# Fused matmul, GELU, matmul by fast bilinear products: issuing the x transposes of block 2 earlier and reordering the sums that read them

## Chip, cores and metric

The kernel runs on one core of one Trainium2 chip. The metric is device time in microseconds (us) of one launch. TensorE (PE) multiplies matrices into PSUM, VectorE (DVE) does elementwise work, ScalarE (ACT) does activations and copies, GpSimd (POOL) and SyncE (SP) mostly issue DMAs here.

## What is computed

```python
# x: (16, 512, 768)  w1: (768, 3072)  b1: (3072,)  w2: (3072, 768), all float32
y = np.matmul(x, w1) + b1
y = 0.5 * y * (1.0 + erf(y / np.sqrt(2.0)))
return np.matmul(y, w2).astype(np.float32)
```

x is read as 8192 rows of 768. The first product with its GELU gives g of 8192 x 3072, which goes to DRAM as fp16 (`gd`), and the second product reads it back.

## The kernel before

Both products are made by bilinear schemes that need fewer block products than the plain method: sums and differences of blocks of x (or g) are multiplied with sums and differences of blocks of w1 (or w2), 20 block products to a *unit*, and the results are combined out of PSUM. Each unit is given by tables: `P1_XOPS` and `P1_WOPS` say which sums to make, `P1_ORD` in which order the 20 products run and in which of 6 PSUM chains each accumulates, `P1_OPS` how PSUM values are copied ('C'), combined ('A') and finished ('F', which ends in a GELU on ACT, a tile of g, and a store of it by SP). The `F` variants of the tables are for the first unit of a block.

**Phase 1** handles the first 512 rows with plain matmuls woven into block 0, and the rest in six *blocks* (`BLK`): blocks 0 and 1 take three times 256 rows, blocks 2 to 5 three times 512. A block of 256s has three units, each over two column groups of w1; a block of 512s has six units. Every unit of phase 1 takes PE about 13 us. **Phase 2** (second product) starts near 455 us and keeps PE busy to the end.

The x rows of block *b* reach PE in three steps:

1. **Cast.** POOL issues a DMA that reads 256 rows of x from DRAM and writes them as fp16 to `xd` in DRAM (`x_cast1`, line 643). Such casts wait for a *marker*: a tiny DVE memset (line 371) put behind a named product of PE, which POOL reads first (line 361). So a cast starts when PE has come to that place.
2. **Transpose.** SP issues a DMA transpose of these 256 rows into SBUF (`load_x`, line 684): three for block 1, six for each block of 512s. Two SBUF areas (`O_XA`, `O_XB`) serve the blocks in turn, so the transposes of block *b* must wait for the last product of block *b-2*.
3. **Sums.** DVE makes 13 sums of the transposed thirds (`x_sums`, recorded under line 333 with tile `ar` and 1536 elements for blocks 2 to 5). Sums 1 and 3 need the second third or parts of it, sum 2 the first, sum 4 the second and third. The first sum reads what transposes 3 and 4 bring, the second transposes 1 and 2, the fourth transposes 3 to 6.

The order of instructions on each engine is not written by hand. A small planner (`Sched`) keeps a model clock for every engine and for the DMAs, takes the task that can start first, and emits it. It runs when the program is built; on the chip each engine then follows its fixed order and waits on semaphores. A task's *due* time puts it behind or ahead of others; `order=` names tasks after which it may be emitted; `lag` is the model's pause after a dependence before it can start; and a DMA is modelled to end two microseconds after its bytes have passed. The model's times decide the order, never the running time itself.

In `load_x` the mark behind which transpose *k* of block *b* is emitted is a store of the block before: for block 2, store 2 + 3*k* of block 1. A few lines carry what the change touches:

```python
            m0, dm = {1: (22, 4), 2: (2, 3)}.get(b, (8, 5))
            mark = blk_stores[b - 1][m0 + dm * k:m0 + dm * k + 1]
            ...
                order=mark, nbytes=256 * K * 2, bulk=1, lag=1.0 if b == 2 else 8.0)
```

The casts of block 3 are issued while blocks 1 and 2 run: the places of their markers are the list `at` and, for the last two, the loop under `if b == 2`. `prods[u][i]` is product *i* of unit *u* of the block just recorded. Stores of g share 13 SBUF buffers (`NGST`), PSUM results on their way share 7 (`NV`)[...].

Of the kernel before, what the change touches and what calls it, by code (L numbers as in the profile page):

```python
# [44 lines left out]
LAT = 0.13  # L45
WIN = 30.0
URG = 1.0


class Val:  # L50
    __slots__ = ("pool", "slot", "prods", "left", "last")
# [37 lines left out]


class Task:
    __slots__ = ("eng", "fn", "nd", "outs", "reads", "alloc", "frees", "due", "key", "end",
                 "deps", "nbytes", "bulk", "lag", "lock", "gen")


class Sched:
# [10 lines left out]
        self.port = 0.0  # L107
        self.pe_ideal = 10.0

    def add(self, eng, fn, reads=(), alloc=None, makes=None, after=(), frees=None, due=None, nbytes=0, bulk=0, order=(), lag=LAT, lock=False):  # L110

        t = Task()
        t.eng, t.fn, t.alloc, t.due, t.nbytes = eng, fn, alloc, due, nbytes
        t.bulk = bulk
        t.lag = lag
        t.lock = lock
        t.end = None
        t.gen = False
        self.key += 1
        t.key = self.key  # L120
        t.outs = []
        t.reads = list(reads)
        t.frees = list(reads) if frees is None else list(frees)
        for v in t.frees:
            v.left += 1
        if makes is None:
            makes = [alloc] if alloc is not None else []
        deps = set(after)
        for v in t.reads:
            deps.update(v.prods)  # L130
        for v in makes:
            v.prods.append(t)
        t.deps = [d for d in deps]
        t.nd = 0
        for d in list(t.deps) + list(order):
            if d.end is None:
                d.outs.append(t)
                t.nd += 1
        self.left += 1
        if "PE" in eng:  # L140
            self.pe.append(t)
            t.due = self.pe_ideal
            self.pe_ideal += eng["PE"]
        elif t.nd == 0:
            self._ready(t)
        return t
# [20 lines left out]
    def run(self, until=None):  # L167
        drift = 0.0
        while self.left:
            best = None  # L170
            if self.pp < len(self.pe):
                drift = max(self.t["PE"] - self.pe[self.pp].due, 0.0)
            if self.pp < len(self.pe):
                t = self.pe[self.pp]
                if t.nd == 0:
                    r = self._start(t, "PE")
                    if r is not None:
                        best = (r, 0, "PE", t)
            for e in ("DVE", "ACT", "POOL", "SP"):
                fg = None  # L180
                bg = None
                now = self.t[e]
                for t in self.avail[e]:
                    r = self._start(t, e)
                    if r is None:
                        continue
                    if t.due is None:
                        c = (r, t.key, t)
                        if e == "DVE" and "ACT" in t.eng and self.t["ACT"] < r + 0.8 and self.pp > 40:
                            continue  # L190
                        if fg is None or c[:2] < fg[:2]:
                            fg = c
                    elif e != "POOL" and r > t.due + drift - URG:
                        c = (r, t.due - 1e9, t)
                        if fg is None or c[:2] < fg[:2]:
                            fg = c
                    elif e == "POOL" or "POOL" not in t.eng or r > t.due + drift - WIN:
                        if e == "POOL" and len(t.eng) > 1 and r + t.eng[e] > t.due + drift - 0.5:
                            continue
                        c = (r > now + 0.2, t.due, t.key, r, t)  # L200
                        if bg is None or c[:3] < bg[:3]:
                            bg = c
                if bg is not None and (fg is None or bg[3] + 0.5 * bg[4].eng[e] <= fg[0]):
                    c = (bg[3], 1, e, bg[4])
                elif fg is not None:
                    c = (fg[0], 1, e, fg[2])
                else:
                    continue
                if best is None or c[0] < best[0]:
                    best = c  # L210
            assert best is not None, "no task can start"
            r, _, e, t = best
            d = t.eng[e]
            if t.alloc is not None and t.alloc.pool is not None:
                t.alloc.slot = t.alloc.pool.take()
            t.fn(e)
            if t.lock and e != "ACT":
                self.port = r + d
            if t.nbytes:
                self.t[e] = r + d  # L220
                self.dma[t.bulk] = max(self.dma[t.bulk], r + d) + t.nbytes / (270e3, 250e3, 200e3)[t.bulk]
                t.end = self.dma[t.bulk] + 2.0
            else:
                t.end = self.t[e] = r + d
            t.eng = {e: d}
            if e == "PE":
                self.pp += 1
            else:
                for q in self.avail.values():
                    if t in q:  # L230
                        q.remove(t)
            for v in t.frees:
                v.left -= 1
                v.last = max(v.last, t.end)
                if v.left == 0 and v.pool is not None:
                    v.pool.put(v.last + LAT, v.slot)
            for o in t.outs:
                o.nd -= 1
                if o.nd == 0 and "PE" not in o.eng:
                    self._ready(o)  # L240
            self.left -= 1
# [3 lines left out]
def kernel(  # L245
# [9 lines left out]
    B, M, K = x.shape  # L255
# [38 lines left out]
    def a32(off, n):  # L294
        return ar[:, off // 2: off // 2 + 2 * n].bitcast(FP32)
# [353 lines left out]
            (j, y) for j in range(3) for y in range(0, n, 256))]  # L649

    for h in range(3):
        gate = [(w1f[2], a32(O_WF + 2 * 6144, 2))] if h == 0 else []
        x1l.append(S.add({"POOL": 0.95}, lambda e, h=h, gate=gate: gated(gate, lambda: nc.gpsimd.dma_start(
            out=a16(O_XN + 6144 + h * 3072, 2 * K).rearrange("p (s k) -> p s k", k=K),
            in_=xr[:, 4 + 2 * h:6 + 2 * h, :])), alloc=x1n[h], reads=[g[0] for g in gate], nbytes=2 * P * K * 4,
            order=x1l[-1:]))
# [19 lines left out]
    def load_x(b):  # L676

        r0, n = BLK[b]
        for k, (j, y) in enumerate((j, y) for j in range(3) for y in range(0, n, 256)):
            a, z = r0[j] + y, r0[j] + y + 256  # L680
            c = xcv[b, k]
            m0, dm = {1: (22, 4), 2: (2, 3)}.get(b, (8, 5))
            mark = blk_stores[b - 1][m0 + dm * k:m0 + dm * k + 1]
            S.add({"SP": 1.6}, lambda e, a=a, z=z, j=j, y=y: nc.sync.dma_start_transpose(
                out=x_third(b, j)[:, :, y:y + 256], in_=xd[a:z, :]), reads=[c], makes=[xsv[b][j], xsv[b][3 + j]],
                after=blk_last[b - 2] if b > 1 else w1op[0] + plain_mm[:8],
                order=mark, nbytes=256 * K * 2, bulk=1, lag=1.0 if b == 2 else 8.0)


    def plain_pair(p):  # L690
# [137 lines left out]
    for b in range(len(BLK)):  # L828
        p1_block(b)
        at = {0: [prods[1][0], prods[1][10], plain_mm[16], plain_mm[20], prods[2][0], prods[2][6]] if b == 0 else [],  # L830
              1: [prods[1][3], prods[1][12], prods[2][3], prods[2][12]]}.get(b, [p[10] for p in prods])
        if b == 2:
            for r, t in zip(x_rows(3)[4:], (prods[0][3], prods[0][12])):
                x_cast1(*r, gate=marker(t), order=poolq)
        if b + 2 < len(BLK):
            for r, t in zip(x_rows(b + 2), at):
                x_cast1(*r, gate=marker(t), order=poolq)
        if b + 1 < len(BLK):
            load_x(b + 1)

        if b == len(BLK) - 2:
            for k in range(12):
                t, h = divmod(k, 2)
                t = (3, 2, 0, 4, 1, 5)[t]
                g = marker(prods[k // 2][(3, 13)[k % 2]])
                poolq.append(S.add({"POOL": 1.0}, lambda e, t=t, h=h, g=g: gated(g, lambda: nc.gpsimd.dma_start(
                    out=w2d[t][:, 4 * h:4 * h + 4, :], in_=w2b[t // 2, t % 2][:, 4 * h:4 * h + 4, :])),
                    reads=[g[0][0]], makes=[], nbytes=2 * P * 1536 * 2, order=poolq[-1:]))
                w2cast[t].append(poolq[-1])
# [192 lines left out]
```

## Time and profile before

| | us |
|---|---|
| median of 13 runs | 885.16 |
| lowest and highest run | 880.65, 893.58 |
| the profiled execution, its own time | 881.16 |
| its span in the trace | 879.4 |
| PE busy | 856.6 |
| DVE busy | 662.4 |
| ACT busy | 447.5 |
| POOL busy | 55.9 |

The trace is of one execution. Its span runs from the first to the last instruction; its own time is 1.8 us longer. "Busy" is the sum of an engine's instructions; idle time of an engine that is not the bottleneck costs nothing. A *releaser* is what ended a wait, inferred from semaphores. In the timelines a bracket holds the idle time of the engine before an instruction and its releaser. A DMA issue on SP or POOL takes the queue's time; its data land later. "PEclk" or "clock" is the share of full speed that TensorE was granted.

### The profile page before, as it was taken

How to read it: one execution, taken by the hardware profiler on the slowest of the kernel's cores; microseconds unless marked ns; L12 is line 12 of the kernel's file. 1: busy time of each engine (PE TensorE's matmuls, PEld its weight loads, DVE VectorE, ACT ScalarE, POOL GpSimd, SP SyncE). 2: the span in 40 equal slices, each digit the busy share in tenths (PEclk: the TensorE clock that was granted, in tenths of full speed). 3: DMA queues.
4: the chain of work that ended last, by engine and by line, in shares of the span. 5: the costliest groups of instructions: out<-in, count | busy, mean ns of one | idle time of the engine just before them, and what ended most of it. 6: DMA issues, size and time to landing. Idle time of an engine off the chain costs nothing.

```text
span 879.4 us, 14440 instructions
## 1 busy us (share of the span) xinstructions
PE 856.6 (97%) x5024; PEld 487.5 (55%) x5024; DVE 662.4 (75%) x1104; ACT 447.5 (51%) x809; POOL 55.9 (6%) x120
## 2 busy tenths in 40 slices
PE   7999979999999999999998999999999999999997
PEld 4766865444444444434445666666666666666664
DVE  3988769688787876797889886687666678666663
ACT  6787858678778777768891222222222222222221
POOL 3101001000000111121100000000000000000000
PEclk9999999999999999999999999999999999999999
DMA  9999798985787699876693546664546665445612
GB/s 257 217 233 198 183 204 184 212 208 154 176 198 193 157 220 233 193 238 206 233 308 116 162 165 216 207 199 155 156 157 205 206 212 168 162 162 169 215 64 72
DMA packets 154312, 166.51 MB, mean 189 GB/s; under 512 B 55504, under 2 KB 146384, under 8 KB 147664
## 3 DMA queue, kind: packets, MB, share of 16 engines
q1 hardware_dynamic: 135040, 134.91, 51.1%
q0 software_dynamic: 16112, 30.68, 19.7%
q8 instruction: 39, 0.64, 0.3%
q10 hardware_dynamic: 3088, 0.01, 0.2%
q14 instruction: 33, 0.27, 0.1%
HBM read 99.10 MB, written 90.83 MB: 216 GB/s over the span
## 4 chain that ended last, share of the span: by engine, by line
PE 85%; DMA 5%; DVE 4%; ACT 3%; issue 2%; SPq 1%; DVEq 0%; ACTq 0%
PE ps L980 47%; PE ps L805 34%; DMA ar<-xd 3%; PE ps L698 3%; DVE vt L333 2%; ACT ar L503 2%; DVE ar L333 1%; DMA ar<-in_w_dram 1%; SPq L508 1%; ACT vt L338 1%; ACT ar L338 0%; DMA gd<-ar 0%; DVE vt L340 0%; DVE vt L331 0%; PE ps L468 0%
## 5 line engine op out<-in xcount | busy, mean ns | idle before, releaser
L980 PE MATMUL ps<-ar 128*128 128x384 f16 x2560 | 416.6, 326 | 2.5 <-DVE vt L333 1.3
L805 PE MATMUL ps<-ar 128*128 128x512 f16 (+1 forms) x2160 | 395.4, 344 | 10.8 <-DVE vt L340 4.8
L980 PEld LDWEIGHTS <-ar 128*128 128x128 f16 x2560 | 250.5, 98 | 168.6 <-issue 3.1
L805 PEld LDWEIGHTS <-ar 128*128 128x128 f16 x2160 | 211.7, 98 | 194.3 <-issue 16.0
L333 DVE TENSOR_TENSOR ar<-ar 128x1024 f16<-128x1024 f16 (+2 forms) x397 | 273.2, 715 | 18.6 <-DMA ar<-xd 11.0
L338 ACT ACTIVATE vt<-ps 128x384 f32<-128x384 f32 (+1 forms) x288 | 151.4, 537 | 266.0 <-PE ps L980 247.0
L333 DVE TENSOR_TENSOR vt<-ps,vt 128x512 f32<-128x512 f32 (+1 forms) x221 | 139.2, 643 | 106.6 <-ACT vt L338 75.3
L503 ACT ACTIVATE ar<-vt,b1t 128x512 f16<-128x512 f32 (+1 forms) x288 | 177.7, 645 | 73.1 <-DVE vt L333 68.2
L333 DVE TENSOR_TENSOR vt<-vt,ps 128x512 f32<-128x512 f32 (+1 forms) x189 | 125.0, 663 | 39.6 <-PE ps L805 24.9
L503 ACT ACTIVATE ar<-ps,b1t 128x512 f16<-128x512 f32 (+1 forms) x168 | 97.5, 619 | 8.4 <-PE ps L698 3.3
L333 DVE TENSOR_TENSOR vt<-vt 128x384 f32<-128x384 f32 (+1 forms) x80 | 48.5, 607 | 12.3 <-ACT vt L338 9.5
L338 ACT ACTIVATE ar<-vt 128x384 f32<-128x384 f32 x32 | 16.7, 523 | 71.7 <-DVE vt L333 71.7
L361 POOL COPY scr<-mkt 1x1 f32<-1x1 f32 x45 | 14.9, 332 | 351.4 <-DVE mkt L371 351.4
L698 PE MATMUL ps<-ar 128*128 128x512 f16 x144 | 33.4, 393 | 2.4 <-DVE ar L340 2.1
L333 DVE TENSOR_TENSOR ar<-vt 128x384 f32<-128x384 f32 x48 | 26.8, 559 | 3.4 <-ACT vt L338 1.2
L331 DVE SCALAR_TENSOR_TENSOR vt<-vt,ps 128x512 f32<-128x512 f32 x30 | 20.6, 686 | 11.5 <-ACT vt L338 9.7
L338 ACT ACTIVATE ar<-ar 128x768 f16<-128x768 f16 (+3 forms) x27 | 24.5, 930 | 5.3 <-DMA ar<-in_x_dram 3.4
L698 PEld LDWEIGHTS <-ar 128*128 128x128 f16 x144 | 14.3, 101 | 20.4 <-issue 2.3
L331 DVE SCALAR_TENSOR_TENSOR ar<-vt,ps 128x384 f32<-128x384 f32 x32 | 17.7, 554 | 5.0 <-PE ps L980 0.7
L340 DVE COPY vt<-ps 128x512 f32<-128x512 f32 x24 | 16.5, 689 | 1.8 <-PE ps L805 1.7
L643 POOL DMA_DIRECT2D xd<-in_x_dram x27 | 13.3, 494 | 5.8 <-issue 3.8
L333 DVE TENSOR_TENSOR ar<-ps,vt 128x384 f32<-128x384 f32 x16 | 8.9, 558 | 4.6 <-PE ps L980 3.3
(25 smaller groups left out, 75.6 us busy)
## 6 DMA issues: line engine op xcount, KB each, us to landing
gd<-ar SPq DMA_DIRECT2D x384, 128.0 KB, 4.0
ar<-gd SPq DMA_DIRECT2D x42, 1024.0 KB, 7.4
out_dram<-ar SPq DMA_DIRECT2D x128, 192.0 KB, 3.6
xd<-in_x_dram POOLq DMA_DIRECT2D x27, 384.0 KB, 6.5
ar<-gd POOLq DMA_DIRECT2D x6, 1024.0 KB, 6.2
w2d<-in_w_dram POOLq DMA_DIRECT2D x12, 384.0 KB, 6.8
ar<-w2d POOLq DMA_DIRECT2D x12, 384.0 KB, 5.4
ar<-in_w_dram SPq DMA_DIRECT2D x4, 768.0 KB, 9.1
```

Of the source, the lines that this page charges most:

```text
L331: eng.scalar_tensor_tensor(out=o, in0=a, scalar=-1.0, in1=b, op0=ALU.mult, op1=ALU.subtract)
L333: eng.tensor_tensor(out=o, in0=a, in1=b, op=ALU.add if op == "+" else ALU.subtract)
L338: nc.scalar.activation(out=o, in_=a, func=ACTF.Copy, scale=float(sg))
L340: eng.tensor_copy(out=o, in_=a)
L361: nc.gpsimd.tensor_copy(out=o[0:1, 0:1], in_=ap[0:1, 0:1])
L503: ft.append(S.add({"ACT": act_ps(n)}, lambda e, y=y: nc.scalar.activation(out=a16(O_GST + g.slot * 1024 + y * n * 2, n), in_=src[1]()[:, y ...
L508: stores.append(S.add({"SP": 0.45}, lambda e: nc.sync.dma_start(out=gd[un][:, t:t + k, c0:c0 + n], in_=a16(O_GST + g.slot * 1024, 512).rea ...
L643: gate, lambda: nc.gpsimd.dma_start(out=xd[a:z, :], in_=xf[a:z, :])),
L698: nc.tensor.matmul(out=ps[:, bv.slot, :], lhsT=a16(O_WS[u // 2] + q * 3072 + kc * 512 + u % 2 * 256, P), rhs=a16(O_XT0 + kc * 1024, 512), ...
L805: nc.tensor.matmul(out=ps[:, bk, y * n:(y + 1) * n], lhsT=w1_ap(u + y, w, kt), rhs=xa[:, kt * n:(kt + 1) * n], start=(first and kt == 0 an ...
L980: nc.tensor.matmul(out=ps[:, bk, 0:NB], lhsT=xa[:, j, :], rhs=a16(w2v[w][j // 4].slot + j % 4 * NB * 2, NB), start=(first and j == 0), sto ...
```

## The change

Three constants are added, and the planner's tasks get a field for how long after its bytes a DMA is modelled to end.

- The transposes of block 2 are marked by the last store of block 0 (the first two), then by stores 1, 3, 5 and 7 of block 1, where before it was stores 2, 5, 8, 11, 14 and 17. Their model lag goes from 1.0 to 0.5.
- The model lets a transpose of block 2 end 8 us after its bytes, of blocks 3 and later 12 us, where it was 2. It moves the sums in DVE's order.
- The casts of block 3 are gated by seven places of which the first is dropped: three in block 1's units 1 and 2, three in block 2's units 0 and 1, where it was four and two.

```diff
+M2 = 2
+L2 = 8.0
+L3 = 12.0
...
-                t.end = self.dma[t.bulk] + 2.0
+                t.end = self.dma[t.bulk] + t.late
...
-        gate = [(w1f[2], a32(O_WF + 2 * 6144, 2))] if h == 0 else []
+        gate = [(w1f[1], a32(O_WF + 6144, 2))] if h == 0 else []
...
             mark = blk_stores[b - 1][m0 + dm * k:m0 + dm * k + 1]
+            if b == 2:
+                mark = (blk_stores[0][-1:] + blk_stores[1])[M2 * max(k - 1, 0):][:1]
...
-                order=mark, nbytes=256 * K * 2, bulk=1, lag=1.0 if b == 2 else 8.0)
+                order=mark, nbytes=256 * K * 2, bulk=1, lag=0.5 if b == 2 else 8.0, late=(0, 2.0, L2)[b] if b < 3 else L3)
...
-              1: [prods[1][3], prods[1][12], prods[2][3], prods[2][12]]}.get(b, [p[10] for p in prods])
+              1: [prods[1][12], prods[2][3], prods[2][12]]}.get(b, [p[10] for p in prods])
         if b == 2:
-            for r, t in zip(x_rows(3)[4:], (prods[0][3], prods[0][12])):
+            for r, t in zip(x_rows(3)[3:], (prods[0][3], prods[0][12], prods[1][3])):
                 x_cast1(*r, gate=marker(t), order=poolq)
```

The instruction orders that the two programs are built to: PE's and POOL's are the same in both. On SP the six transposes of block 2 stand, counted in stores of g after block 0's last one, behind 0, 1, 2, 5, 9 and 12 stores, where it was 3, 6, 9, 12, 15 and 18. On DVE the sums of blocks 2 to 4 stand elsewhere among the evictions of PSUM; ACT takes one w1 copy and one PSUM copy from DVE.

One line belongs to none of these parts: at the start POOL reads a word of a piece of w1, which SP loads in four pieces (line 416), before it issues its first load of x (line 653). With the change it reads the second piece instead of the third.

More of the change, by code (lines that the diff above doesn't have):

```diff
@@ L91 @@
 class Task:
-    __slots__ = ("eng", "fn", "nd", "outs", "reads", "alloc", "frees", "due", "key", "end",
+    __slots__ = ("eng", "fn", "nd", "outs", "reads", "alloc", "frees", "due", "key", "end", "late",
                  "deps", "nbytes", "bulk", "lag", "lock", "gen")
@@ L108, in __init__, with add @@
         self.pe_ideal = 10.0
-    def add(self, eng, fn, reads=(), alloc=None, makes=None, after=(), frees=None, due=None, nbytes=0, bulk=0, order=(), lag=LAT, lock=False):
+    def add(self, eng, fn, reads=(), alloc=None, makes=None, after=(), frees=None, due=None, nbytes=0, bulk=0, order=(), lag=LAT, lock=False, late=2.0):
         t = Task()
@@ L116, in add @@
         t.lock = lock
+        t.late = late
         t.end = None
```

## The prediction

> **What bounds the kernel now.** I began with busy time: TensorE (PE) works 97% of the span, so only moments in which its queue stands still, or its clock is cut, can be won. The page's chain of waits has three things beside matmuls that this change touches: `DMA ar<-xd` 3%, `DVE ar L333` 1% and `SPq L508` 1%. Next I asked who waited for whom between 116 and 126 us, where block 1's third unit starts:
>
> ```profile
> PEld L805 <- issue: 5.0, 1, 5.0
> PE ps L805 <- DVE vt L340: 4.8, 1, 4.8
> DVE ar L333 <- DMA ar<-xd: 4.2, 1, 4.2
> ```
>
> PE stood 4.8 us for a VectorE (DVE) copy, and DVE stood 4.2 us for a transpose of x. DVE's timeline there (start, length, what, idle before):
>
> ```profile
> 113.43 0.69 DVE L333 TENSOR_TENSOR vt<-ps,vt 128x512 f32<-128x512 f32 x1
> 115.93 0.69 DVE L333 TENSOR_TENSOR vt<-vt,ps 128x512 f32<-128x512 f32 x1 [1.81 <-PE ps L805]
> 120.83 1.83 DVE L333 TENSOR_TENSOR ar<-ar 128x1536 f16<-128x1536 f16 x2 [4.21 <-DMA ar<-xd]
> ...
> 123.77 0.95 DVE L333 TENSOR_TENSOR ar<-ar 128x1536 f16<-128x1536 f16 x1
> 124.65 0.68 DVE L340 COPY vt<-ps 128x512 f32<-128x512 f32 x1
> ```
>
> The two instructions at 120.83 are x sums of block 2, which no matmul needs for another 16 us (the third unit's 13.1 us from 117.6, with the stall and the slow clock, end near 137). Behind them in DVE's queue is the copy that PE needs. The SyncE (SP) queue's timeline shows why the transpose was late:
>
> ```profile
> 97.05 3.67 SPq L508 DMA_DIRECT2D gd<-ar  x4
> 100.89 1.41 SPq L684 DMA_TRANSPOSE ar<-xd  x1
> 102.39 1.55 SPq L508 DMA_DIRECT2D gd<-ar  x3
> 104.05 1.41 SPq L684 DMA_TRANSPOSE ar<-xd  x1
> ...
> 107.23 1.43 SPq L684 DMA_TRANSPOSE ar<-xd  x1
> ...
> 110.40 5.41 SPq L684 DMA_TRANSPOSE ar<-xd  x1
> ```
>
> The sums wait for the fourth transpose, issued at 110.40. Pieces of the chain of waits, in order of time:
>
> ```profile
> 78.31 11.13 PE ps L805 x102
> ...
> 110.40 10.33 DMA ar<-xd
> ...
> 125.39 6.36 PE ps L805 x42
> ```
>
> It took 10.33 us. After the stall 42 matmuls took 6.36 us; at the rate before it (11.13/102 = 0.109 us) they take 4.58, so 1.78 us more went to a slow clock. The busy times by stage agree (length, PE, PEld, DVE, ACT, POOL, then clock, DMA share, GB/s):
>
> ```profile
> 104.50:117.60 13.10, 13.08 (x121) 11.57 (x120) 8.99 (x16) 10.41 (x27) 1.32 (x4) 1.00 1.10 193
> 117.60:130.70 13.10, 8.29 (x63) 6.61 (x61) 8.10 (x13) 5.51 (x14) 0.66 (x2) 0.87 1.04 217
> ```
>
> DMA issues between 101 and 108 us (transposes alone with stores), then between 108.5 and 115.5 (casts of block 3 beside them; the first line of that is the casts' queue):
>
> ```profile
> ar<-xd SPq DMA_TRANSPOSE x3, 4.2
> ```
> ```profile
> q0 software_dynamic: 32, 0.39, 44.4%
> ...
> ar<-xd SPq DMA_TRANSPOSE x2, 8.7
> ```
>
> Landing takes 4.2 us without a cast, 8.7 beside one.
>
> **What the skill says.** The Trainium skill, "TensorE: Matmul & The Clock Gate", Part 1: after an idle window of about 3.4 us the clock is halved for at least one window. The trace agrees: clock 0.87 over 13.1 us is 3.4 us at half speed. "DMA: Bandwidth & Descriptors", Queues, rings and completion order: an engine alternates between queues packet by packet. A large packet then holds small ones up; the casts' 32 packets for 0.39 MB, and 8.7 against 4.2 us, fit this. "PSUM — Partial Sum Buffer", Engine vs sequencer instructions: VectorE's queue is strictly first in, first out; above, ready evictions stood behind the waiting sums.
>
> **The change part by part.** I also compared the two built instruction orders: PE's and POOL's are the same, so the casts move by their markers alone.
>
> 1. *Transposes of block 2 on SP.* The store at 97.05 is block 0's last; three stores then stood ahead of the first transpose. Now it goes at 97.55 (97.05 and 0.5 for one store). The tile it overwrites is free: block 0's last unit, 120 matmuls of 0.109 us from 78.31, ends near 91.4. A transpose costs SP 1.5 us (1.41 and the gap), a store 0.53 (1.55/3 and the gap). The new order has 5 stores before the fourth transpose and 12 before the sixth: 97.55 + 3x1.5 + 5x0.53 = 104.7 us and 97.55 + 5x1.5 + 12x0.53 = 111.4 us, against 110.40 and 122.80. At 4.2 us the fourth lands near 109. The engines are nearly full: six transposes (0.39 MB) and 12 stores (0.13 MB) are 3.9 MB, and 101 to 108 us moved 211 GB/s, hence 18.6 us from 97.6: the sixth lands at 115.6 to 116.5. Stores passed by a transpose leave 1 to 4.5 us later. That is hidden by the 13 g buffers: ScalarE (ACT) fills one per 1.1 us (12 per unit of 13.1 us), a reserve of 14 us, against up to 4.5 of delay and about 3 of landing (2.9 in that window). If the reserve were used up, ACT would wait, then DVE's buffers, then PE, us for us.
>
> 2. *Casts of block 3.* The one at 108.63 goes; from 113.9 on, each gate serves the cast before it, and a sixth falls into block 2's second unit. Block 3's first transpose starts at 153.0 and the sixth at 184.0, the last moved cast lands near 155 (its gate lies 3 products into a unit that starts near 145; landing 6.7): nothing waits, nor the stores behind on SP. What is left is the cast at 113.9, which can still meet the sixth transpose: 4.5 us (8.7 less 4.2), at most 121.
>
> 3. *Sums on DVE.* Same 13 sums per block (0.87 us each back to back). In block 1 the first two now stand one eviction earlier, right after the one at 113.43, so they need the fourth transpose at 114.1: 5 us of reserve. Then: two sums to 115.9, eviction to 116.6, sum to 117.5, two evictions to 118.8, and the fourth sum, which needs the sixth transpose: expected 116, at most 121, so a hold of 0 to 2.2 us. I take 0.5. The copy goes from DVE to ACT, which does three in a row there; in the trace that pattern after seven sums in one boundary cost PE 0.87 us (140.40 to 141.26). It stays at block 2's start, and at this boundary, with six sums, I put 0 to 0.9, taken 0.3.
>
> 4. *Later blocks.* The first sums of blocks 3 and 4 come a unit (13 us) later. In before they held DVE for 6.8 us (11.0 for all six waits on `ar<-xd`, less 4.2) in five small waits, but PE showed no gap there. Gain in the profiled execution 0; in others, where a transpose lands later, up to a few us. They are packed 3, 4, 5 to a unit: 4x0.87 = 3.5 us against 4.1 us that DVE has free in a unit (13.1 less 8.99), so it fits. Block 5's sums move nearly not at all.
>
> 5. *Gate of the first x load on POOL.* It waits for w1's second piece (landed 13.24) instead of the third (15.50), so POOL's three x loads and the w1 loads behind them start 2.26 us earlier, while the third and fourth pieces are still in flight. The x loads landed at 21.4, 23.8 and 26.5, and PE transposed them at 25.0, 26.6 and 28.1 without a gap: nothing to win. The third piece, cast by DVE at 15.83, may come up to a us later; PE takes it up near 18.7, ready near 16.4 before, so 1 us of delay is covered. The fourth (18.70, cast at 20.87) has 2 us. I take 0, from 0 to 0.8.
>
> 6. One w1 copy goes from DVE (0.35 us) to ACT (0.84 us) near 59 us; ACT idles 0.9 us there: nothing; without that gap, 0.84 us at most.
>
> Sum for the profiled execution (881.16 us; span 879.4): -4.80 - 1.78 + 0.5 + 0.3 = -5.8, hence 875.4; bounds 874.6 (no new waits) and 880.2 (2.2, 0.9, 0.8 and another half-clock window of 1.7). The median of the runs is 4.0 above the profiled one. I let half of this surplus go, since late transposes are its likely cause and part 4 gives them a unit more: 875.4 + 2 = **877.4 us**. If all of it stays, 879.4.
>
> **Rivals.**
> A, as above, 0.74: 873 to 880 at the median. The lower end is 874.6 less the 0.87 gap, should it go, and the 0.5 by which the fastest run (880.65) undercuts the profiled one.
> B, the wait moves: the sixth transpose lands with the 10.33 us of the worst one, at 121.7; DVE stands 2.9 us, PE about as long, and pays a half window: 881.16 - 6.6 + 2.9 + 1.7 = 879.2, 883 at the median. For it: the cast at 113.9 is still there. Against: most of that transpose's packets are ahead of the cast's. 0.12, half of it within the bound.
> C, slower: DVE falls behind. Sums packed 3, 4, 5 into the last units before blocks 3 and 4 make evictions late, and PE waits at both starts and at block 2's. It decides once DVE's free 4.1 us in a unit are overdrawn by about 2 us (a store pass or an ACT delay would do): 3 x (2 + 1.7 for the clock) = 11, so 881.2 - 5.8 + 11 = 886, 890 at the median. For it: the 0.87 us gap after seven sums. Against: block 2's first unit took ten sums and lost just that. 0.08.
> D, nothing arrives earlier, as the DMA engines are full anyway: 881, median 885. Against: from 101 to 108 us slices at 340 GB/s stand beside slices under 100, so there is room. 0.06.
>
> **Numbers.** About 0.5% (4.4 us) is what a measurement can tell from no change. Faster: 0.71 of A and half of B, 0.77; same: 0.03, 0.06 and D's 0.06, 0.15; slower 0.08. The range 873 to 882 takes A and the faster half of B.
>
> **What would show it.** Right: the first transpose of block 2 near 97.6, the fourth landing before 114; no PE gap near 120; a clock of 1.00 between 117 and 131; DVE's wait on `ar<-xd` falling from 11.0 us to under 3. Wrong: a DVE wait on the sixth transpose over 2 us near 119, or PE gaps over 1 us at the starts of blocks 2 to 4.

## The result

| | before | after |
|---|---|---|
| median, us | 885.49 | 874.89 |
| lowest and highest run | 879.93, 898.65 | 873.51, 876.47 |
| the profiled execution, its own time | 881.16 | 875.95 |
| its span | 879.4 | 874.1 |

The medians are of all 48 and 11 runs; the ratio leaves out every run more than 1.5% above the fastest of its kernel. It is 0.9884 (after to before), with a 95% interval of 0.9861 to 0.9907. The forecast was 877.4 us (873 to 882) at the median and 875.4 for the profiled execution. Two things happened: a stall went, and so did nearly all of the spread. The runs of before cover 19 us, those of after 3. Long runs became rare, though, and did not vanish: of six later runs of after one took 881.32 us.

### The profile after

First the waits between 113 and 124 us, where before had the 4.8 us stall (columns: engine, line waited for, releaser; then us in total, times, longest):

```profile
PEld L811 <- issue: 1.2, 2, 1.0
PE ps L811 <- ACT vt L342: 0.8, 1, 0.8
```

TensorE's wait is 0.8 us, and it is now for a ScalarE copy. The line `DVE ar L333 <- DMA ar<-xd`, 4.2 us in that stretch before, has no successor, and none is left in the list for the whole span. The DVE timeline shows why:

```profile
113.51 0.69 DVE L337 TENSOR_TENSOR vt<-ps,vt 128x512 f32<-128x512 f32 x1
114.12 1.82 DVE L337 TENSOR_TENSOR ar<-ar 128x1536 f16<-128x1536 f16 x2
116.01 0.69 DVE L337 TENSOR_TENSOR vt<-vt,ps 128x512 f32<-128x512 f32 x1
116.61 0.95 DVE L337 TENSOR_TENSOR ar<-ar 128x1536 f16<-128x1536 f16 x1
...
119.29 1.83 DVE L337 TENSOR_TENSOR ar<-ar 128x1536 f16<-128x1536 f16 x2
```

The two sums that stood from 116.62 to 120.83 start at 114.12 without a wait, and the fourth sum (the first of the pair at 119.29) also finds its data. SP's queue shows when they were brought:

```profile
95.46 1.41 SPq L690 DMA_TRANSPOSE ar<-xd  x1
...
104.57 1.63 SPq L690 DMA_TRANSPOSE ar<-xd  x1
...
111.68 2.28 SPq L690 DMA_TRANSPOSE ar<-xd  x1
```

These are the first, fourth and sixth transpose. The fourth landed at 108.73, 5.4 us ahead of the sum that reads it, the sixth at 116.47, 2.8 us ahead. The unit after that boundary has its clock back (busy us by engine as before, clock, DMA share, GB/s):

```profile
117.70:130.80 13.10, 12.29 (x112) 10.72 (x110) 11.94 (x19) 11.00 (x28) 1.87 (x4) 1.00 0.92 210
```

112 matmuls in 13.1 us instead of 63, at clock 1.00 instead of 0.87.

Where the 5.2 us between the two profiled executions came from can be read by taking the start of the *n*th matmul in both traces and subtracting. After is 5.86 us ahead at 150 us: 4.80 of stall and 1.78 of slow clock, less the new 0.79. It is 6.14 ahead just before 181, falls back to 4.32 there, and is 5.25 ahead at 338. So some 0.3 and 0.9 us more came, in four pieces of 0.3 to 0.4 us, each some 5 us behind one of the waits for a transpose that before had in blocks 3 to 5 (at 175.58, 189.09, 253.84 and 332.19). One new stall took 1.8 back. It is in the waits between 165 and 178 us:

```profile
ACT ar L507 <- DMA gd<-ar: 2.5, 1, 2.5
...
PE ps L811 <- ACT vt L342: 1.7, 1, 1.7
```

ScalarE had no free g buffer, as a store had not landed, and the PSUM copies behind it on ScalarE were late. POOL's timeline shows what ran beside the stores (the markers' reads and one cast are left out):

```profile
154.28 0.49 POOL L647 DMA_DIRECT2D xd<-in_x_dram  x1 [0.27 <-issue]
...
155.62 0.49 POOL L647 DMA_DIRECT2D xd<-in_x_dram  x1
...
167.23 0.49 POOL L647 DMA_DIRECT2D xd<-in_x_dram  x1 [0.27 <-issue]
```

With the one at 154.88 between, that is three casts in 1.4 us: the moved one of block 3 runs into the first ones of block 4. The second transpose of block 3 then held SP's queue for 5.90 us instead of 1.4, and stores stood behind it; one issued at 167.06, beside the cast at 167.23, landed at 173.92 after 6.86 us, and the GELU at 174.01 is the one that waited. But the three casts alone do not make this stall. After, run again, had them too (154.56, 155.16 and 155.90), and a transpose held SP's queue for even 7.80 us; yet the store in the same place, issued at 166.31 and so 1.2 us ahead of the next cast, landed after 3.94 us, and TensorE had no gap there.

### The profile page after: what moved, and what is told of

Read it like the earlier page. It is cut to its first block, busy times and chain, and to the rows that moved or that the text cites. A ratio compares the mean times of both kernels' runs of the same rounds, so it can differ in the third digit from the quotient of the medians.

```text
span 874.1 us, 14442 instructions
## 1 busy us (share of the span) xinstructions
PE 854.0 (98%) x5024; PEld 486.6 (56%) x5024; DVE 661.9 (76%) x1102; ACT 448.7 (51%) x811; POOL 56.3 (6%) x120
## 3 DMA queue, kind: packets, MB, share of 16 engines
HBM read 99.10 MB, written 90.83 MB: 217 GB/s over the span
## 4 chain that ended last, share of the span: by engine, by line
PE 91%; ACT 3%; DMA 2%; DVE 2%; issue 1%; SPq 0%; DVEq 0%; ACTq 0%
PE ps L986 48%; PE ps L811 40%; PE ps L704 3%; ACT ar L507 2%; DMA gd<-ar 1%; DMA ar<-in_w_dram 1%; DVE vt L337 1%; DVE ar L337 1%; ACT vt L342 1%; DMA ar<-xd 0%; ACT ar L342 0%; DVE vt L335 0%; SPq L391 0%; PE ps L472 0%; PE ps L483 0%
```

## The experiments

The change has three parts that can move time: the marks (transposes of block 2 issued early), the late order (`L2` for block 2, `L3` for later blocks: sums placed as if transposes landed late) and the casts. The gate is a fourth. Edits are shown against before where the label says "only", else against after.

| kernel | median | lowest, highest | ratio to before, 95% interval |
|---|---|---|---|
| marks only | 888.03 | 882.29, 906.09 | 1.0032, 1.0005 to 1.0058 |
| casts only | 884.53 | 879.69, 898.55 | 0.9999, 0.9971 to 1.0026 |
| late order only (L2 and L3) | 880.67 | 875.97, 882.83 | 0.9933, 0.9912 to 0.9954 |
| L3 only | 880.86 | 875.17, 884.46 | 0.9965, 0.9946 to 0.9984 |
| after with L3 = 2 | 882.22 | 876.01, 892.69 | 0.9972, 0.9945 to 0.9998 |
| after, casts as before | 874.62 | 874.34, 879.30 | 0.9908, 0.9873 to 0.9943 |
| after, marks as before | 875.18 | 874.11, 877.56 | 0.9893, 0.9841 to 0.9945 |
| after, gate as before | 874.95 | 874.12, 884.94 | 0.9883, 0.9853 to 0.9913 |
| after, casts spread | 874.52 | 873.55, 876.94 | 0.9904, 0.9868 to 0.9939 |
| the last, and L2 = 10 | 876.13 | 873.50, 878.42 | 0.9896, 0.9848 to 0.9945 |
| after again | 874.16 | 873.14, 881.32 | 0.9886, 0.9833 to 0.9938 |

Each ratio is to runs of before on the same chip, reckoned as in the result. The medians are of all runs and come from different chips, so two rows are best compared by their ratios and intervals.

### Marks only

```diff
-            mark = blk_stores[b - 1][m0 + dm * k:m0 + dm * k + 1]
+            if b == 2:
+                mark = (blk_stores[0][-1:] + blk_stores[1])[M2 * max(k - 1, 0):][:1]
...
+                lag=0.5 if b == 2 else 8.0
```

> Only the marks of block 2's transposes are changed; model ends, casts and gate are as before. SyncE issues them as in the changed kernel (first near 95 to 98 us), but the sums stand earlier in VectorE's order (four sums around the start of block 1's third unit, the fourth wanted near 117.5 us) and the cast at 108.6 is back. Theory 1 (the place in SyncE's queue is what cost 6.6 us): the fourth transpose lands by 112, the 4.8 us gap near 120 is under 1 us, time 876 to 879. Theory 2 (the order of the sums is needed too): VectorE stands 1 to 4 us for the sixth transpose near 118, PE gap 1 to 3 us there, time 879 to 883.

It was no faster than before: 888.03 us, at a ratio whose interval lies just above 1 and is within 0.6% of it. In its profile the stall did not go, it grew. Waits between 112 and 127 us:

```profile
PE ps L811 <- ACT vt L342: 5.5, 1, 5.5
DVE ar L337 <- DMA ar<-xd: 4.6, 1, 4.6
```

The DVE timeline names the sum, and SP's the transpose:

```profile
122.00 0.96 DVE L337 TENSOR_TENSOR ar<-ar 128x1536 f16<-128x1536 f16 x1 [4.57 <-DMA ar<-xd]
```
```profile
111.92 5.74 SPq L690 DMA_TRANSPOSE ar<-xd  x1
```

The fourth transpose landed at 108.74, as early as in after, and the first two sums went through. But the planner, which believes in a landing after 2 us, now put the fourth sum just behind the third (116.48), where it must have the sixth transpose. That one was issued at 111.92, held SP's queue for 5.74 us beside a cast, and landed at 121.98. This is the prediction's rival B, in full. The stage table shows its price in clock; the second line is of the last 3.4 us of the slow stretch:

```profile
117.60:130.70 13.10, 7.60 (x50) 5.70 (x49) 7.39 (x11) 5.78 (x13) 1.21 (x2) 0.77 0.89 192
128.03:131.44 3.41, 3.41 (x18) 2.35 (x17) 1.70 (x4) 0.29 (x1) 0.00 (x0) 0.50 0.19 38
```

0.77 over 13.1 us is 6 us at half speed (13.1 x 0.23 x 2), and the slow stretch goes on past the end of that row: from 124.62 to 131.44 it is 6.8 us, twice the 3.4 us in before's profile. So earlier transposes alone are no gain: the order of the sums eats what they bring.

### Casts only

```diff
-              1: [prods[1][3], prods[1][12], prods[2][3], prods[2][12]]}
+              1: [prods[1][12], prods[2][3], prods[2][12]]}
...
-            for r, t in zip(x_rows(3)[4:], (prods[0][3], prods[0][12])):
+            for r, t in zip(x_rows(3)[3:], (prods[0][3], prods[0][12], prods[1][3])):
```

> Only the casts of block 3 are moved on; the cast at 108.6 us is gone, SyncE's order and the modelled ends are as before. Theory 1 (the cast beside the third and fourth transpose made them slow): the third lands near 111.5 and the fourth near 114.6 instead of 114.3 and 120.7, no hold of VectorE near 116, gap near 120 under 1 us, time 876 to 879. Theory 2 (the place in SyncE's queue made them late): the fourth lands at 118 or later, gap 2 us or more, time 882 to 885.

With the cast at 108.63 out of the way the fourth transpose, issued as late as before, landed at 114.64 instead of 120.7. So it was the cast that made it take 10.33 us. The other profiles agree: with the transposes as late as before it took 10.33 to 12.16 us in the four that have this cast, and 4.69 and 4.84 in the two that don't. DVE waited 0.7 us for it, and TensorE's gap at that place was 0.30 us. Yet the median, 884.53, cannot be told from before. In the profile the gain was given back at block 3's start. Waits between 160 and 182 us, and from the timelines TensorE's gap and DVE's wait:

```profile
DVE ar L337 <- DMA ar<-xd: 3.8, 1, 3.8
ACT ar L507 <- DMA gd<-ar: 3.7, 2, 2.2
...
PE ps L809 <- ACT vt L342: 2.0, 1, 2.0
```
```profile
177.50 3.12 PE L809 MATMUL ps<-ar 128*128 128x512 f16 x9 [2.01 <-ACT vt L342]
178.12 1.83 DVE L337 TENSOR_TENSOR ar<-ar 128x1536 f16<-128x1536 f16 x2 [3.80 <-DMA ar<-xd]
```

With the model's 2 us, the sums of block 3 stand where their transposes may not have come: DVE stood 3.8 us for the fourth, which landed at 178.10. But TensorE's gap of 2.01 us had ended before that, at 177.50. TensorE waited there for a ScalarE copy, and ScalarE was late because it had stood 2.24 and 1.45 us for g buffers: stores had landed late (the one issued at 158.03 only at 169.37). So here the loss came mostly by way of the stores. Three casts stood side by side in that stretch too, and the second transpose, issued at 154.10, landed only at 169.10. A half-clock window followed at 178.4.

### Late order only, and L3 only

```diff
-                t.end = self.dma[t.bulk] + 2.0
+                t.end = self.dma[t.bulk] + t.late
...
+                late=(0, 2.0, L2)[b] if b < 3 else L3
```

with `L2 = 8.0`, `L3 = 12.0`:

> Only the modelled end of the transposes is changed (8 and 12 us); they are issued as late as before and the cast at 108.6 is there. Only one sum stands near the start of block 1's third unit instead of three, the rest comes later. Theory 1 (transposes must come earlier): the fourth lands near 120 as before; the gap near 120 goes, since no sum stands ahead of the copy, but up to 3 us come back at the start of block 2, where eleven sums crowd: 878 to 882. Theory 2 (the order alone is enough): 875 to 877, and the spread of the runs falls from some 19 us to under 5.

and with `L2 = 2.0`, `L3 = 12.0`:

> The kernel before with one thing changed: the modelled end of the transposes of blocks 3 to 5 is 12 us instead of 2, so their sums stand later in VectorE's order. Block 2 and the casts are as before, so the stall near 120 us (4.8 us and a slow clock window, 6.6 in all) stays. Theory 1 (the spread of the runs comes from late transposes of blocks 3 to 5): median 879 to 882, the runs within 6 us of each other or little more. Theory 2 (the spread comes from block 2's stall, whose length varies): median 884 to 886 with a spread of 15 us or more.

Both came to 881 us. Both intervals lie below 1, but the gain of L3 alone by its ratio, 0.35%, is under the 0.5% that the prediction set as what a measurement can tell. Its effect on the long runs is plain: none of its 22 took over 884.46 us, where 14 of 31 runs of before on that chip took over 890. In its profile the gap that begins at 120.75 stays (4.53 us), and blocks 3 to 5 show none. With L2 as well, no sum stands ahead of the copy near 120 (the first comes at 121.29, the fourth transpose landed at 120.89), but a gap of 3.79 us comes at block 2's start instead. It is no wait for x. SP's timeline there:

```profile
118.10 3.05 SPq L688 DMA_TRANSPOSE ar<-xd  x1
...
122.92 4.02 SPq L688 DMA_TRANSPOSE ar<-xd  x1
127.04 15.50 SPq L512 DMA_DIRECT2D gd<-ar  x15
```

The last two transposes held the queue for 3.05 and 4.02 us, and behind the last one 15 stores went out without a pause: a backlog. ScalarE then stood for g buffers (2.8 us in two waits between 130 and 145 us) with PSUM copies queued behind; the store it stood for longest was issued at 127.66, beside a cast issued at 127.71, and took 6.15 us to land. A late transpose thus has two ways to TensorE: through the sums on DVE, and through the stores on SP. L2 closed the first here and left the second open.

### After with L3 = 2

```diff
-L3 = 12.0
+L3 = 2.0
```

> The changed kernel with the modelled end of the transposes of blocks 3 and later back at 2 us (block 2's stays at 8). The sums of blocks 3 to 5 stand a unit earlier, as before. Theory 1 (the spread of the runs before, 880 to 899, came from late transposes of blocks 3 to 5 that held VectorE): median 876 to 880 and a spread of over 6 us; VectorE waits for transposes 5 to 8 us in all. Theory 2 (the spread came from block 2's stall alone): median and spread as the changed kernel, 874 to 876 and about 3 us.

882.22 us: in the changed kernel the later order of blocks 3 to 5 is worth 7.3 us by the medians, 0.9% by the ratios (0.9884 against 0.9972, whose intervals don't touch), and the spread is back (876 to 893). DVE and PE at block 5:

```profile
333.64 1.83 DVE L337 TENSOR_TENSOR ar<-ar 128x1536 f16<-128x1536 f16 x2 [6.01 <-DMA ar<-xd]
```
```profile
337.92 4.28 PE L811 MATMUL ps<-ar 128*128 128x512 f16 x13 [3.97 <-DVE vt L344]
```

DVE stood 6.01 us for the fourth transpose of block 5, TensorE 3.97 for the copy behind, and a half-clock window came with it. In before's profile the same two sums stood 1.67 us and cost no gap; in after they come a whole unit later (338.52) and wait for nothing.

### Marks as before, casts as before, gate as before

After with one part undone in each, by the reverse of the diffs above; for the gate:

```diff
-        gate = [(w1f[1], a32(O_WF + 6144, 2))] if h == 0 else []
+        gate = [(w1f[2], a32(O_WF + 2 * 6144, 2))] if h == 0 else []
```

> The changed kernel with the marks of block 2's transposes back behind stores 2, 5, 8, 11, 14 and 17 of block 1 (casts, gate and modelled ends as in the changed kernel). The first goes near 100 instead of 95.5 us, the sixth lands near 123. Theory 1 (with the sums ordered late, the early issue still matters, since block 2's sums otherwise crowd at its start): PE gaps of 2 to 4 us near the start of block 2, time 877 to 880. Theory 2 (the order of the sums and the missing cast carry it all): 874 to 876.

> The changed kernel with the casts of block 3 gated as before: one falls near 108.6 us again, and only two instead of three follow each other near 150. Theory 1 (the cast near 108.6 delays the fifth and sixth transpose): the sixth lands at 119 to 122, the fourth sum holds VectorE 0 to 2 us, time 875 to 878. Theory 2 (moving the casts mostly costs, since three of them in a row near 154 held stores back and ScalarE waited 2.5 us for a g buffer): the 1.66 us gap near 175 goes and the time is 872 to 874.5.

> The changed kernel with the gate of the first x load back on the third piece of w1. Theory 1 (the gate is worth nothing): 874 to 876. Theory 2 (it is part of the gain or a cost): over 1 us away from 874.9.

None of the three loses anything that these few runs can tell. In the first the transposes of block 2 are issued from 100.29 to 120.00, as late as before; the fourth landed at 115.1 and the sixth at 124.1, and no gap is near 120. The moved cast alone would have taken most of it away, as casts only shows (0.30 us); the order adds room. The DVE timeline:

```profile
118.27 0.68 DVE L337 TENSOR_TENSOR vt<-vt,ps 128x512 f32<-128x512 f32 x1
118.87 0.69 DVE L344 COPY vt<-ps 128x512 f32<-128x512 f32 x1
119.47 0.95 DVE L337 TENSOR_TENSOR ar<-ar 128x1536 f16<-128x1536 f16 x1
...
121.41 0.95 DVE L337 TENSOR_TENSOR ar<-ar 128x1536 f16<-128x1536 f16 x1
```

All evictions that TensorE needs, the copy at 118.87 included, stand ahead of the first sum, which starts at 119.47 with 4 us in hand. With the casts as before instead, the sixth transpose landed at 121.0, DVE waited 0.8 us for it, and TensorE had one gap of 1.75 us near 122, a clock of 1.00 behind it, and the same median. So, with the late order in place, early marks and a moved cast seem to stand in for each other: either one, added to the late order, goes with medians of 875 instead of 880.7, and both bring no more. The profiles say the same, as neither has the 3.79 us gap and the half-clock window of the late order alone; the intervals of the ratios, though, still overlap.

### Spreading the casts, a later L2, and two repeats

```diff
-              1: [prods[1][12], prods[2][3], prods[2][12]]}.get(b, [p[10] for p in prods])
+              1: [prods[1][12], prods[2][3], prods[2][12]],
+              2: [prods[1][12], prods[2][6], prods[2][16]] + [p[10] for p in prods[3:]]}.get(b, [p[10] for p in prods])
...
-            for r, t in zip(x_rows(3)[3:], (prods[0][3], prods[0][12], prods[1][3])):
+            for r, t in zip(x_rows(3)[3:], (prods[0][3], prods[0][12], prods[0][18])):
```

This pulls the three casts at 154.28 to 155.62 apart (to 147.33, 155.82 and 167.32). The second kernel adds `L2 = 10.0`, against the 0.79 us at block 1's third unit. Before and after were run again unchanged.

> The changed kernel with the last cast of block 3 and the first three of block 4 gated one after the other (product 18 of block 2's unit 0, product 12 of unit 1, products 6 and 16 of unit 2) instead of three at almost the same time. Theory 1 (the three casts in a row near 154 us held stores back, and the 1.66 us gap near 175 follows from that): no two casts within 4 us, ScalarE does not wait for a g buffer there, the gap goes, time 872.5 to 874. Theory 2 (the gap comes from the order of the evictions there): the gap stays, time 874.5 to 876.

> The kernel with the casts one after the other, and in addition the modelled end of block 2's transposes at 10 us instead of 8, so that three instead of six sums stand around the start of block 1's third unit and two more in block 2's first unit. Theory 1 (the 0.79 us gap near 120.5 comes from sums ahead of evictions and with that of ScalarE's copies): that gap goes, nothing comes in its place, 873 to 874.5. Theory 2 (the sums moved back make a gap at block 2's start): 0.5 to 2 us there, 874.5 to 876.

> The changed kernel unchanged, on the same chip as the three beside it, to compare them with: 873.5 to 876.5.

> The kernel before, unchanged, one more profile: its runs lie between 880 and 904 us and the profile at hand was taken at the low end (881.2). Theory 1 (late transposes of blocks 3 to 5 make the slower runs): if this execution is above 884, PE shows gaps of over 1 us near 175 to 195, 250 to 270 or 330 to 340, with VectorE waiting for a transpose just before. Theory 2: the gap near 120 is longer than 4.8 us by what the run is slower.

With the casts spread, the gap at 175 is gone. But the unchanged kernel, profiled again, has no such gap either, so this run settles nothing: the gap, of 1.7 us, is one of that execution and not of every one. L2 = 10 left 0.84 us at 119.70, so that gap isn't one of the sums' place alone, and its profile has 2.4 us at 187 behind a wait for g buffers. Neither differs from after by what can be measured. No kernel here beats after.

Before again (883.87) shows one source of the spread. Waits between 113 and 128 us:

```profile
PE ps L805 <- DVE vt L340: 6.2, 1, 6.2
DVE ar L333 <- DMA ar<-xd: 5.6, 1, 5.6
```

The same program stood 6.2 us here instead of 4.8, and its clock fell to 0.77 between 117.6 and 130.7, where it was 0.87. TensorE had no gap over 0.7 us in blocks 3 to 5, so the 2.7 us by which this run is longer came at this stall: 1.4 us more of gap, and 3.4 us more at half speed. That late transposes of blocks 3 to 5 make long runs too rests on the runs with and without L3; no run of before over 890 us was profiled.

## Why the prediction was right, and where it was off

The direction, the range and the profiled execution (875.4 forecast, 875.95 measured) were right; the median came 2.5 us below the forecast.

**Step 1, transposes on SP.** The fourth was forecast to issue at 104.7 and land near 109, the sixth to issue at 111.4 and land at 115.6 to 116.5. Measured: 104.57 and 108.73; 111.68 and 116.47. The first went at 95.46, not at 97.55: block 0's last store, at 97.05 in before's profile, went at 94.84 here. A store at 99.10 then held the queue for 2.29 us, so that the fourth kept to its time is partly luck. And that the transposes' *earliness* is what wins was wrong: marks alone gained nothing, and after without the marks lost nothing.

**Step 2, casts.** "nothing waits, nor the stores behind on SP" failed in the profiled execution. I had the last moved cast land near 155. DVE ran its marker only at 153.62, together with the next one, so it was issued at 154.28 and landed at 160.13, with two casts of block 4 right behind it. A transpose beside them held SP's queue for 5.90 us, and TensorE lost 1.7 after it. I looked for who reads the cast's result, not for what its packets run beside. After again had the same three casts and lost nothing there, so how much of the 1.7 is theirs stays open.

**Step 3, sums.** The hold for the sixth transpose, taken as 0.5, was 0; the gap at this boundary, taken as 0.3, was 0.79; the 0.87 us at block 2's start stayed (134.87 to 135.74). The two errors cancel to 0.01, by luck. The fit of the profiled execution, 0.55 us, is in part luck as well: the 1.8 us lost near 175 and the 1.2 us gained in small pieces were both forecast as 0.

**Step 4, later blocks: the step that failed.** "I let half of this surplus go" was the mis-sized term. The surplus was the 4.0 us by which before's median lay over its profiled run; after's median lies 1.1 *below* its own. All of it went. The cause that I named was right, and L3 is worth 7.3 us by the medians in the changed kernel. But I read its price from one execution, where waits of 1.0 to 1.7 us at blocks 3, 4 and 5 happened to open no visible gap, and I wrote that "Block 5's sums move nearly not at all". Its first two move by a whole unit (so not only the sums of blocks 2 to 4 stand elsewhere), and after with L3 = 2 stood 6.01 us at just those.

**Steps 5 and 6.** The gate was put at 0 (to 0.8): 874.95 without it, so 0. The w1 copy wasn't tried alone; the profile shows no gap there.

**The rivals.** B's mechanism is real: marks only is B, at a 5.5 us gap where I priced 2.9, and at 6.8 us of half clock where I priced 3.4. The late order and the moved cast kept it out of after: with the casts as before, its remnant is 1.75 us. C did not come: DVE kept up with the sums packed later. D fell with step 1's landings.

**Open.** Marks, casts and L3 together without L2 were not tried, so it is not shown that after needs L2. Beside L3 alone it brought nothing that can be told (medians 880.67 and 880.86, ratios 0.9933 and 0.9965 with intervals that overlap); in the profile the stall moved to the stores. Nor were the moved casts and L3 alone, without marks and L2. They may be enough: casts only had no stall near 120, and its loss lay at block 3. Which block's late transposes weigh most over many executions, and why landings differ from one execution to the next, is open too.

## What to carry to other kernels

Where work that waits for a DMA shares an in-order queue with evictions that the bottleneck needs, place it by the *latest* landing seen, not by the usual one: lateness that costs nothing in one profile costs several us in other runs. Bringing the data sooner doesn't replace this, as a planner that believes in early data moves the waiting work forward with it. A spread of runs far wider than the profile explains is itself a finding, and worth forecasting apart from the profiled execution.

## What the runs showed of the hardware

- A transpose beside a cast does not only land late, it can also hold SP's queue. Block 2's fourth took 10.3 to 12.2 us to land and held the queue for 5.1 to 5.5 us in the four profiles in which it goes near 110 and a cast near 108.7 (before, before again, late order only, L3 only). Where it goes near 110 without that cast (casts only; after, marks as before), it took 4.7 and 4.8 us and held the queue for 1.4. Other transposes beside casts held it for anything from 1.3 to 8.2 us. Stores behind one that holds it long are late, whoever reads the transpose.
- The clock's price comes in windows of 3.41 us. In every trace the slow stretches last 3.41 or 6.83 us, and in the one trace with two of them (marks only) they begin 215.04 us apart, which is 63 times 3.413. Half speed came after such a window if TensorE had stood still in it for 1.9 us (the kernel with L2 = 10, gap of 2.37 us at 187), 2.0 (casts only, gap of 2.01 at 175), 2.3 (marks only, gap of 2.48 at 337) or longer; it did not come after gaps of 0.8 to 1.75 us, even where two windows running had 1.1 and 1.5 us of standstill (after with L3 = 2, 173.4 to 180.2). Gaps of 3.79 to 4.80 us brought one window at half speed, gaps of 5.5 and 6.2 us two, as 1.4 and 2.2 us of them fell into the first slow window. So it matters where a gap falls, and not only how long it is. The Trainium skill, "TensorE: Matmul & The Clock Gate", Part 1, puts the idle window at about 3.4 us. The length of the window agrees; the idle time that brings half speed on does not, as 1.9 us in a window were enough, and the measurements decide.
